# A second block's input projection in pairs of column blocks with seven products, and an SSM projection with its weights stationary

## The chip, the cores and the metric

The kernel runs on one core of a Trainium2 chip. The metric is the device time of one execution in microseconds, the median of several runs. The core has five engines with queues of their own that meet through semaphores: TensorE (PE; its weight loads are listed apart as PEld), VectorE (DVE), ScalarE (ACT), GpSimd (POOL) and SyncE (SP), which here only issues DMAs.

## The reference

Two transformer-like blocks run one after the other on 1024 tokens of width 1024, all in float32. Inputs are x, a conditioning vector and some forty weights.

The first block normalises and modulates x, projects it with `w_in`, and runs a dilated attention and a state-space branch (SSM) beside each other. The 256 SSM input columns are a slice of that projection. Both branches are gated, merged and projected, and a convolutional feed-forward layer follows.

The second block is the one that matters here:

```python
h = _rmsnorm_2(x, norm_g)
p = h @ w_in                      # 1024 x 1024 times 1024 x 7680
(u, v, z_a, x_b, b_g, c_g, z_b, x_c, z_c, g_a, g_b, g_c) = split(p)
y_a = (gmlp(u, layernorm(gelu(v))) * silu(z_a)) @ w_pa
y_b = (shortconv(x_b, b_g, c_g) * silu(z_b)) @ w_pb
y_c = (pool(x_c) * silu(z_c)) @ w_pc
merged = sigmoid(g_a) * y_a + sigmoid(g_b) * y_b + sigmoid(g_c) * y_c
out = _rmsnorm_2(x + merged @ w_o, final_g)
```

`shortconv` multiplies c_g by x_b, runs a causal convolution of width 3 over tokens and multiplies by b_g. `pool` takes causal window means of 2, 4, 8 and 16 tokens over four groups of 128 columns. `gmlp` mixes tokens in chunks of 128 with a triangular matrix per group.

## The kernel before

Precision: every float32 operand X of a large product is split into a high part (`hi`, a cast by ACT to a rounded float32 format) and a low part (`lo`, X minus hi, a subtraction on DVE or POOL). A product is three matmuls: hi·hi, hi·lo and lo·hi. `split` does this for activations and `Stream.split_to` for weights.

Layouts: `mmB` holds 128 weight columns stationary and moves 512 tokens past them, so that its result has features on partitions; a block is 8 row tiles of the contraction, 3 passes and 2 token halves, 48 matmuls. `mmA` holds 128 tokens stationary and moves 512 weight columns.

Order: the kernel is not issued as it is written. `Plan.add` (L212) records every operation, and `Plan.schedule` (L277) is a list planner: it keeps a model clock with a price for each operation (`Plan.cost`, L249), lets every engine take the first operation in the order of writing that is ready and whose buffers fit, and so fixes the order on each engine and the place of each buffer. All operations are issued at L432, so each row of the profile has that line. There are 50 SBUF tiles of 128 x 1024 ("s"), two PSUM tiles of two banks ("mm") and four of one ("tr"). Groups of buffers have caps in `nc.glim`: 5 raw weight tiles ("r") and 14 split ones ("w").

Weights: `_items` lists the weight tiles of 512 KB in the order of use. `Stream.dma_to` loads them on SP's queue, `split_to` splits them, `get` hands them out.

The stages that the change touches are these:

- "us", the SSM input projection, before the gates of the first block. For each of eight token phases it takes every eighth token as the stationary operand (a slice with a step of 8) and moves 256 weight columns: 8 x 8 x 3 matmuls. DVE copies the result to `xs`, and `ssm_gen` goes on from there, a few steps after each gate.
- "lastdown": the last feed-forward projection of the first block, its normalisation in batches of four token tiles, and `u3_tr`, the transposes to features on partitions for the second block. The first token half is transposed during the last tiles, the second during the next stage. `x2_out` sends the block's output to DRAM for the last residual.
- "A_v", "A_uz": v, u and z_a with `mmA`; gelu, layernorm and products per token tile. "spat": the token mixing and 32 transposes.
- "gateA", "B", "gateB", "C", "zc", "gc", "yc": column blocks one by one with `mmB`; each gate block is followed by its part of an output projection (`gated`), so that the gates stay in SBUF.
- "wo": the output projection, with the residual added in `proj_half`, and the last normalisation.

Of the kernel before, what the change touches and what calls it, by code (L numbers as in the profile page):

```python
# [19 lines left out]
NT = 8  # L20
# [26 lines left out]
NWARM = 14  # L47
WPOOL = set([0, 1, 2, 3])
# [20 lines left out]

def _items():  # L70
# [3 lines left out]
    for k in range(2):  # L74
        it.append(("U", "w_in", k, 1536, 256))
# [32 lines left out]
    for nm in ("v", "u", "za"):  # L108
        for k in range(4):
            it.append(("A", "w_in_2", k, o[nm], 512))  # L110
    it.append(("WS", None, 0, 0, 0))
    for n in range(0, 8, 2):
        it.append(("B", "w_in_2", n, o["ga"], 128))
        it.append(("B", "w_in_2", n + 1, o["ga"], 128))
        it.append(("P", "w_pa_2", n, 0, 0))
    for n in range(4):
        for nm in ("cg", "xb", "bg", "zb"):
            it.append(("B", "w_in_2", n, o[nm], 128))
    for n in range(0, 8, 2):
        it.append(("B", "w_in_2", n, o["gb"], 128))  # L120
        it.append(("B", "w_in_2", n + 1, o["gb"], 128))
        it.append(("P", "w_pb_2", n, 0, 0))
    for n in range(4):
        it.append(("B", "w_in_2", n, o["xc"], 128))
    it.append(("WP", None, 0, 0, 0))
    for n in range(4):
        it.append(("B", "w_in_2", n, o["zc"], 128))
    for n in range(8):
        it.append(("B", "w_in_2", n, o["gc"], 128))
    for n in range(0, 8, 2):  # L130
        it.append(("P", "w_pc_2", n, 0, 0))
# [13 lines left out]
class Plan:  # L145
# [103 lines left out]
    def cost(self, eng, method, args, kw):  # L249
# [198 lines left out]
def kernel(ctx: ExitStack, tc: tile.TileContext, x, wts, wada, vecs, rows, ssmv, wglu, ttab, iden,  # L448
# [11 lines left out]
    nc.glim = {"r": 5, "w": 14}  # L460
# [8 lines left out]
    def raw():  # L469
        return slot("r", group="r")  # L470
# [19 lines left out]
    mod = nc.own(cst.tile([128, 32], F32, name="mod"), "cst", 99)  # L490
    half = nc.own(cst.tile([128, 2], F32, name="half"), "cst", 99)
# [15 lines left out]
    x2_d = dtile("x2_d", 8)  # L507

# [57 lines left out]
    class Stream:  # L566
# [6 lines left out]
        def dma_to(self, j):  # L573
            while self.d <= min(j, len(_ITEMS) - 1):
                t = raw()
                w = _item_cols(_ITEMS[self.d])
                nc.sync.dma_start(out=t[:, :w], in_=wts[self.d][:, :w])
                self.raw[self.d] = t
                self.d += 1

        def split_to(self, j):
            while self.s <= min(j, len(_ITEMS) - 1):
                self.dma_to(self.s)
                r = self.raw.pop(self.s)
                it = _ITEMS[self.s]
# [10 lines left out]
                self.s += 1  # L596

# [60 lines left out]
    def wA(items):  # L658
        return [p for i in items for p in wA1(i)]

# [642 lines left out]
    wu = []  # L1303
    for _ in range(2):
        h, l = st.get()
        hv, lv = kview(h, 4, 256), kview(l, 4, 256)
        for k in range(4):
            wu.append((hv[:, k, :], lv[:, k, :]))
    xs = [slot("xs"), slot("xs")]
    for q in range(2):  # L1310
        ps = mm_ps()
        for j in range(4):
            s = 4 * q + j
            ws_ = []
            for k in range(8):
                h, l = u.full[k]
                ws_.append((h.rearrange("p (j s) -> p s j", s=8)[:, s, :], l.rearrange("p (j s) -> p s j", s=8)[:, s, :]))
            mmA(ps[:, 256 * j:256 * j + 256], ws_, wu)
        p3 = ps.rearrange("p (s g c) -> p s g c", s=4, g=16)
        for gh in range(2):  # L1320
            nc.vector.tensor_copy(out=xs[gh].rearrange("p (g s c) -> p s g c", g=8, s=8)[:, 4 * q:4 * q + 4],
                                  in_=p3[:, :, 8 * gh:8 * gh + 8, :])
# [276 lines left out]
    def proj_half(a, c, src, dst, row):  # L1599
# [4 lines left out]
        for t in range(NT):  # L1604
# [4 lines left out]
            if row is None and c and t == NT - 1:  # L1609
                for c_ in (slice(0, 256), slice(256, 512)):  # L1610
                    ps = tr_ps()[:, 0:256]
                    mmA(ps, xs, [(h[:, c_], l[:, c_]) for h, l in w])
                    tt(o[:, c_], ps, xr[:, c_], ALU.add)
# [4 lines left out]
            if row is None:  # L1618
                tt(o, ps, xr[:, 0:512], ALU.add)
# [166 lines left out]
    x2_of = {}  # L1786

    def x2_out(t):
        a, r = x2_of.pop(t)
        x2 = slot("x2")  # L1790
        act(x2, a, AF.Identity, scale=r)
        nc.gpsimd.dma_start(out=x2_d[t], in_=x2)

    def u3_tr(th, k):
        if (k, th) not in u.half:
            u.half[k, th] = slot("u3", F32R).rearrange("p (h n) -> p h n", h=2)
        o = u.half[k, th]
        tr_evac([xn[4 * th + j] for j in range(4)], k, o[:, 0, :], o[:, 1, :], vec("norm_g_2", k))

    for t in range(NT):  # L1800
# [13 lines left out]
        if j == 3:  # L1814
# [7 lines left out]
            ra, rb = r[:, 0:4], r[:, 4:8]  # L1822
            for jj in range(4):
                a = xn[t - 3 + jj]
                n_ = slot("xn")
                if XL[jj] == "a":
# [4 lines left out]
                x2_of[t - 3 + jj] = (a, ra[:, jj:jj + 1])  # L1831
        if t in (4, 5, 6, 7):
            u3_tr(0, 2 * (t - 4))
            u3_tr(0, 2 * (t - 4) + 1)
            x2_out(t - 4)
    del g2r, gfr, w
    fts.clear()
    nc.label = "A_v"

    lnr = slot("lnr")  # L1840
    load_in(lnr, rows[4].partition_broadcast(128))
    wv = wA([st.get() for _ in range(4)])
    vh = [slot("vh", F32R) for _ in range(4)]
    vl = [slot("vl", F32R) for _ in range(4)]
# [319 lines left out]
```

## Time and profile before

| | |
|---|---|
| median of 3 runs | 2172.23 us (2171.98 to 2172.95) |
| profiled execution | 2172.54 us |
| its span, from first to last instruction | 2170.8 us |
| instructions in the span | 24273 |
| PE busy, matmuls | 2119.2 us (98%), 9774 |
| PEld busy | 1764.2 us (81%) |
| DVE busy | 1141.4 us (53%) |
| ACT busy | 653.2 us (30%) |
| POOL busy | 267.6 us (12%) |
| mean granted clock of TensorE | 0.987 |

Busy times are of the span. A matmul's own duration in the listings covers its way through the array, and neighbours overlap; how fast they follow each other is read from a group's busy time over its count. In an operation, "s" is any SBUF tile, "mm" and "tr" are the PSUM tiles, "sm" small tiles; "out<-in" names what is written and read.

### The profile page before, as it was taken

How to read it: one execution, taken by the hardware profiler on the slowest of the kernel's cores; microseconds unless marked ns; L12 is line 12 of the kernel's file. 1: busy time of each engine (PE TensorE's matmuls, PEld its weight loads, DVE VectorE, ACT ScalarE, POOL GpSimd, SP SyncE). 2: the span in 40 equal slices, each digit the busy share in tenths (PEclk: the TensorE clock that was granted, in tenths of full speed). 3: DMA queues.
4: the chain of work that ended last, by engine and by line, in shares of the span. 5: the costliest groups of instructions: out<-in, count | busy, mean ns of one | idle time of the engine just before them, and what ended most of it. 6: DMA issues, size and time to landing. Idle time of an engine off the chain costs nothing.

```text
span 2170.8 us, 24273 instructions
## 1 busy us (share of the span) xinstructions
PE 2119.2 (98%) x9774; PEld 1764.2 (81%) x9774; DVE 1141.4 (53%) x1897; ACT 653.2 (30%) x947; POOL 267.6 (12%) x280
## 2 busy tenths in 40 slices
PE   6999989999999999999999999999999999999998
PEld 4798868888888788888887878888888888888887
DVE  8858764887673852444347587431232232540445
ACT  4402213776522433112112374221111111221312
POOL 4202421222301100000004225000000000000020
PEclk9999979999999999999999999999999999999999
DMA  8518134433652321211122221210111111111212
GB/s 322 179 67 273 68 107 107 107 85 81 251 176 83 122 88 39 78 39 59 49 88 88 68 107 49 76 60 30 59 49 39 39 58 43 51 49 39 92 54 78
DMA packets 60224, 195.15 MB, mean 90 GB/s; under 512 B 6992, under 2 KB 11440, under 8 KB 60112
## 3 DMA queue, kind: packets, MB, share of 16 engines
q1 hardware_dynamic: 40464, 136.39, 18.4%
q0 software_dynamic: 19648, 57.22, 8.2%
q8 instruction: 76, 1.25, 0.2%
q14 instruction: 36, 0.29, 0.0%
HBM read 156.29 MB, written 28.31 MB: 85 GB/s over the span
## 4 chain that ended last, share of the span: by engine, by line
PE 91%; DVE 7%; issue 1%; DMA 0%; ACT 0%; POOL 0%; SPq 0%; DVEq 0%; ACTq 0%; POOLq 0%
PE mm L432 59%; PE tr L432 32%; DVE s L432 6%; DVE sm L432 1%; ACT s L432 0%; POOL s L432 0%; DMA s<-in_wada_dram 0%; DMA gs_d<-s 0%; DVE mod L432 0%; SPq L432 0%; DVEq L432 0%; ACTq L432 0%; POOLq L432 0%
## 5 line engine op out<-in xcount | busy, mean ns | idle before, releaser
L432 PE MATMUL mm<-s,s 128*128 128x512 f32 (+1 forms) x5960 | 1381.9, 392 | 4.1 <-DVE s L432 2.0
L432 PEld LDWEIGHTS mm<-s,s 128*128 128x128 f32 x5960 | 1130.0, 194 | 230.3 <-DVE s L432 4.6
L432 PE MATMUL tr<-s,s 128*128 128x512 f32 (+4 forms) x3192 | 700.5, 377 | 12.9 <-DVE s L432 11.1
L432 PEld LDWEIGHTS tr<-s,s 128*128 128x128 f32 (+2 forms) x3192 | 561.6, 190 | 122.2 <-DVE s L432 14.0
L432 DVE TENSOR_TENSOR s<-s,s 128x1024 fp32r<-128x1024 f32 (+12 forms) x387 | 416.4, 1100 | 287.9 <-PE mm L432 223.2
L432 ACT CAST s<-s 128x1024 fp32r<-128x1024 f32 (+4 forms) x238 | 217.6, 933 | 351.7 <-DVE s L432 123.7
L432 ACT ACTIVATE s<-s 128x512 f32<-128x512 f32 (+4 forms) x139 | 120.8, 869 | 397.3 <-DVE s L432 317.7
L432 POOL TENSOR_TENSOR s<-s,s 128x512 fp32r<-128x512 f32 (+11 forms) x106 | 166.3, 1583 | 294.5 <-ACT s L432 205.8
L432 DVE SCALAR_TENSOR_TENSOR s<-s,mm 128x1024 f32<-128x1024 f32 x48 | 58.6, 1220 | 161.6 <-PE mm L432 114.7
L432 DVE SCALAR_TENSOR_TENSOR s<-s,s 128x1024 fp32r<-128x1024 f32 (+4 forms) x65 | 79.5, 1225 | 98.9 <-ACT s L432 98.5
L432 DVE TENSOR_TENSOR s<-tr,s 128x512 fp32r<-128x512 f32 (+3 forms) x114 | 72.5, 652 | 99.7 <-PE tr L432 77.2
L432 ACT ACTIVATE s<-s,sm 128x512 f32<-128x512 f32 (+7 forms) x127 | 99.4, 798 | 66.5 <-DVE sm L432 66.1
L432 ACT ACTIVATE s<-mm 128x1024 f32<-128x1024 f32 x32 | 32.9, 1028 | 259.8 <-PE mm L432 259.8
L432 PE MATMUL tr<-idn,s 128*128 128x128 f32 x560 | 83.7, 282 | 16.6 <-ACT s L432 10.4
L432 POOL DMA_DIRECT2D s<-x_d x16 | 8.8, 549 | 722.0 <-PE mm L432 721.4
L432 PEld LDWEIGHTS tr<-idn,s 128*128 128x128 f32 x560 | 68.3, 144 | 33.3 <-ACT s L432 12.9
L432 DVE TENSOR_TENSOR s<-s,tr 128x512 f32<-128x512 f32 (+1 forms) x130 | 78.8, 618 | 27.1 <-PE tr L432 19.3
L432 DVE SCALAR_TENSOR_TENSOR s<-mm,vt,s 128x1023 f32<-128x1023 f32 (+3 forms) x36 | 41.8, 1162 | 82.2 <-ACT s L432 81.7
L432 DVE TENSOR_TENSOR s<-s,mm 128x1024 f32<-128x1024 f32 (+1 forms) x26 | 29.6, 1137 | 89.0 <-PE mm L432 88.6
L432 ACT COPY s<-tr 64x256 f32<-64x256 f32 (+2 forms) x78 | 37.2, 485 | 45.4 <-PE tr L432 24.5
L432 ACT ACTIVATE s<-mm,hb 128x1024 f32<-128x1024 f32 x15 | 16.7, 1115 | 105.3 <-PE mm L432 82.0
L432 ACT ACTIVATE s<-tr 128x512 f32<-128x512 f32 (+1 forms) x44 | 25.9, 595 | 72.9 <-PE tr L432 66.9
(100 smaller groups left out, 669.8 us busy)
## 6 DMA issues: line engine op xcount, KB each, us to landing
s<-in_wts_dram SPq DMA_DIRECT2D x167, 512.0 KB, 3.7
s<-in_wada_dram SPq DMA_DIRECT2D x48, 512.0 KB, 6.1
s<-s POOLq DMA_DIRECT2D x32, 256.0 KB, 4.9
s<-in_x_dram SPq DMA_DIRECT2D x8, 512.0 KB, 9.1
v_d<-s POOLq DMA_DIRECT2D x8, 512.0 KB, 5.7
gs_d<-s POOLq DMA_DIRECT2D x8, 512.0 KB, 4.2
ga_d<-s POOLq DMA_DIRECT2D x8, 512.0 KB, 3.2
s<-in_ttab_dram SPq DMA_DIRECT2D x8, 512.0 KB, 3.9
```

Of the source, the lines that this page charges most:

```text
L432: hook(getattr(getattr(self.nc, eng), method)(*args, **kw), self.ops[i][7] + f"|{self.start[i]:.0f}|{i}")
```

## The change

Column blocks of `w_in_2` go through the second block in 30 pairs. A pair is two blocks of 128 columns, B1 and B2; the contraction of 1024 is cut into two halves and the tokens into two halves. So the product is a 2 x 2 by 2 x 2 block product, and it is done in Winograd's form of Strassen's scheme with seven products of a 512-row contraction instead of eight. The operands of activations (a11, a12, s1 to s4, a22; `Seven`) are made once. Those of weights (b11, b21, t1 to t4, b22; `Weights`) are made for each pair: POOL adds, ACT and DVE split. A product is 4 row tiles x 3 matmuls of 512 tokens. `seven` puts them together: some results are copied or added by ACT and DVE into two output tiles, and three products are accumulated onto what already stands in their PSUM bank.

The first three pairs do their two products of the first token half early (`first_halves`), before the second half is transposed. v, u and z_a now also come with features on partitions: v is transposed for its layernorm (`ln_gen`, run in steps between the pairs of "B"), and "spat" multiplies after its transposes. The gates, the branches b and c and the normalised v go to DRAM (`g2_d`, `bb_d`, `cc_d`, `vq_d`) and come back for the three output projections, which now stand at the end, one after the other. The block's output for the residual goes to DRAM unscaled, and `proj_half` scales it when it adds it.

The "us" stage uses `mmB` (two blocks of 48 matmuls with weights stationary), copies the result to SBUF and transposes it: 16 transposes that read tokens with a step of 8.

The planner's price of such a matmul goes from n/2.4 + 2.5 to (n + 32)/2.4 ns, and the caps "rr" (6 raw tiles of paired weights), "w2" (9 weight operands) and "o" (6 output tiles) are new. Raw tiles of pairs are not loaded earlier than 120 operations ahead.

```diff
@@ Plan.cost
-                return (n if n >= 256 else 4 * n) / 2.4 + 2.5
+                return ((n if n >= 256 else 4 * n) + 32) / 2.4
@@ "us"
-    for q in range(2):
-        ps = mm_ps()
-        for j in range(4):
-            s = 4 * q + j
-            ws_ = []
-            for k in range(8):
-                h, l = u.full[k]
-                ws_.append((h.rearrange("p (j s) -> p s j", s=8)[:, s, :], l.rearrange("p (j s) -> p s j", s=8)[:, s, :]))
-            mmA(ps[:, 256 * j:256 * j + 256], ws_, wu)
+    for gh in range(2):
+        ps = mm_ps()
+        mmB(ps, wB(st.get()), u, 8)
+        f = slot("us")
+        for h in range(2):
+            c = slice(512 * h, 512 * h + 512)
+            nc.scalar.copy(out=f[:, c], in_=ps[:, c])
+        ...
+                nc.tensor.transpose(out=ps[:, 128 * j:128 * j + 128],
+                                    in_=f.rearrange("p (j s) -> p s j", s=8)[:, 4 * h + j, :], identity=idn)
+            nc.vector.tensor_copy(out=x4[:, 4 * h:4 * h + 4], in_=ps.rearrange("p (s g c) -> p s g c", s=4, g=8))
@@ class Seven
+        def rest(self, ps, qs):
+            for k in ks:
+                p, q, n = ps[k], qs[k], ns[k]
+                v.tensor_tensor(out=lo(n), in0=lo(q), in1=hi(q), op=ALU.add)
+                v.tensor_tensor(out=hi(n), in0=lo(n), in1=lo(p), op=ALU.subtract)
+                put("s2", k, hi(n), v)
+                g.tensor_tensor(out=lo(q), in0=lo(p), in1=lo(q), op=ALU.subtract)
+            for k in ks:
+                put("s3", k, lo(qs[k]), g if k < 2 else v)
+            for k in ks:
+                put("s1", k, lo(ns[k]), v)
+                g.tensor_tensor(out=hi(ps[k]), in0=hi(ps[k]), in1=hi(ns[k]), op=ALU.subtract)
+            for k in ks:
+                put("a22", k, hi(qs[k]), v)
+            for k in ks:
+                put("s4", k, hi(ps[k]), g)
@@ products
+    def product(X, W, key, ps, a, b, on):
+        wh, wl = W.pop((key, b))
+        for k in range(X.nk):
+            xh, xl = X.p[a, k]
+            c = slice(128 * k, 128 * k + 128)
+            for i, (l_, r_) in enumerate(((wh, xh), (wh, xl), (wl, xh))):
+                nc.tensor.matmul(out=ps, lhsT=l_[:, c], rhs=r_, start=not on and not k and not i, ...)
+    def halves(X, W, key):
+        o1 = slot("o1", group="o")
+        pa = tr_ps()
+        product(X, W, key, pa, "a11", "b11", False)
+        nc.scalar.copy(out=o1[:, 512:1024], in_=pa)
+        yield o1
+        product(X, W, key, pa, "a12", "b21", True)
+        nc.scalar.copy(out=o1[:, 0:512], in_=pa)
+    def seven(X, W, key, o1=None):
+        ...
+        product(X, W, key, pb, "s2", "t2", False)
+        tt(c12, c21, pb, ALU.add)
+        if g:
+            next(g, None)
+        pc, pd = mm_ps()[:, 0:512], mm_ps()[:, 0:512]
+        product(X, W, key, pc, "s3", "t3", False)
+        tt(c22, c12, pc, ALU.add)
+        product(X, W, key, pd, "s1", "t1", False)
+        tt(c22, c22, pd, ALU.add)
+        product(X, W, key, pc, "a22", "t4", True)
+        tt(c21, c12, pc, ALU.add)
+        product(X, W, key, pd, "s4", "b22", True)
+        tt(c12, c12, pd, ALU.add)
+        return o1, o2
@@ start of the second block
+    pre = first_halves(X, W, range(NPRE))
+    for k in range(4):
+        u3_tr(1, k)
+    X.rest([xq[k] for k in range(4)], [xq2[k] for k in range(4)])
@@ gates
+    def gate_pairs(gd):
+        for n in range(0, 8, 2):
+            for j, g in enumerate(pair()):
+                act(g, g, AF.Tanh, scale=0.5)
+                nc.gpsimd.dma_start(out=gd[n + j], in_=g)
@@ proj_half
-                tt(o, ps, xr[:, 0:512], ALU.add)
+                stt(o, xr[:, 0:512], ra2[:, t:t + 1], ps, ALU.mult, ALU.add)
```

## Rows read from the trace of the kernel before

**Rows 1.** Page: busy us of PE, and the clock strip in 40 slices.
```profile
PE 2119.2 (98%) x9774; PEld 1764.2 (81%) x9774; DVE 1141.4 (53%) x1897; ACT 653.2 (30%) x947; POOL 267.6 (12%) x280
PEclk9999979999999999999999999999999999999999
```

**Rows 2.** Page: chain that ended last, by engine.
```profile
PE 91%; DVE 7%; issue 1%; DMA 0%; ACT 0%; POOL 0%; SPq 0%; DVEq 0%; ACTq 0%; POOLq 0%
```

**Rows 3.** Waits of PE: us in total, times, longest (first, last of eight).
```profile
PE tr L432 <- DVE s L432: 22.5, 12, 7.5
...
PE mm L432 <- DMA s<-in_wada_dram: 0.4, 1, 0.4
```

**Rows 4.** Windows: us, busy PE PEld DVE ACT POOL, PEclk, DMA share, GB/s.
```profile
96.60:142.80 46.20, 46.20 (x194) 46.20 (x194) 20.45 (x148) 3.30 (x4) 0.53 (x1) 1.00 0.39 145
...
1450.00:1700.00 250.00, 250.00 (x1104) 207.02 (x1103) 60.14 (x51) 41.91 (x41) 0.00 (x0) 1.00 0.15 47
...
285.00:335.00 50.00, 41.96 (x154) 32.53 (x152) 22.50 (x26) 9.80 (x12) 8.11 (x8) 0.69 0.34 109
1254.00:1265.00 11.00, 7.92 (x36) 6.47 (x35) 8.56 (x15) 8.70 (x13) 3.74 (x3) 0.84 0.12 48
```

**Rows 5.** Chain in order of time, a piece: start us, us, what.
```profile
848.52 43.52 PE mm L432 x192
```

**Rows 6.** Lines of PE by form, 95:165: count, busy us, mean ns.
```profile
L432 PE MATMUL mm<-s,s 128*128 128x256 f32 x192 | 46.3, 403 | 0.0
```

**Rows 7.** Timeline of PE, 1240:1330: start us, us, instruction, count, idle before.
```profile
1257.47 2.68 PE L432 MATMUL tr<-idn,s 128*128 128x128 f32 x16 [3.08 <-ACT s L432]
...
1266.21 1.03 PE L432 MATMUL tr<-idn,s 128*128 128x128 f32 x8
1267.00 5.73 PE L432 MATMUL mm<-s,s 128*128 128x512 f32 x24
```

**Rows 8.** Lines of DVE by form, whole run (first), then 1350:2150.
```profile
L432 DVE TENSOR_TENSOR s<-s,s 128x512 fp32r<-128x512 f32 x26 | 21.9, 855 | 1.6 <-ACT s L432 1.5
...
L432 DVE TENSOR_TENSOR s<-s,s 128x1024 fp32r<-128x1024 f32 x75 | 91.9, 1237 | 204.0 <-PE mm L432 199.0 <-ACT s L432 4.5
...
L432 DVE TENSOR_TENSOR s<-s,s 128x128 f32<-128x128 f32 x32 | 7.2, 286 | 0.2
...
L432 DVE TENSOR_TENSOR s<-s,tr 128x512 f32<-128x512 f32 x4 | 2.7, 684 | 0.1
```

**Rows 9.** Lines by form, whole run: DVE evacuation, ACT cast, POOL addition, issue.
```profile
L432 DVE TENSOR_SCALAR s<-tr,mod 128x512 f32<-128x512 f32 x16 | 12.5, 806 | 5.0 <-ACT s L432 4.7 <-PE tr L432 0.2
...
L432 ACT CAST s<-s 128x512 fp32r<-128x512 f32 x27 | 16.3, 618 | 8.2 <-DVE s L432 7.6
...
L432 POOL TENSOR_TENSOR s<-s,s 128x512 f32<-128x512 f32 x20 | 28.1, 1417 | 49.5 <-ACT s L432 46.0 <-DVE s L432 3.4
...
L432 POOL DMA_DIRECT2D s<-x_d x16 | 8.8, 549 | 722.0 <-PE mm L432 721.4 <-issue 0.6
```

**Rows 10.** Timeline of DVE: one 512-column low part, and the second half's scaling.
```profile
80.30 0.69 DVE L432 TENSOR_TENSOR s<-s,s 128x512 fp32r<-128x512 f32 x1 [0.71 <-ACT s L432]
...
1287.72 1.42 DVE L432 TENSOR_SCALAR s<-s,sm 128x1024 f32<-128x1024 f32 x2
```

**Rows 11.** Timeline of DVE: two idle times in "us", and the long stretch.
```profile
119.80 1.29 DVE L432 COPY s<-mm 128x512 f32<-128x512 f32 x2 [12.66 <-PE mm L432]
...
142.85 1.29 DVE L432 COPY s<-mm 128x512 f32<-128x512 f32 x2 [12.66 <-PE mm L432]
...
247.89 52.21 DVE L432 TENSOR_TENSOR s<-s,s 128x1008 f32<-128x1008 f32 x38 [1.76 <-POOL s L432]
```

**Rows 12.** Timelines of POOL and DVE about 58, and one DVE addition alone.
```profile
57.71 2.34 POOL L432 TENSOR_TENSOR s<-s,cact 128x1024 f32<-128x1024 f32 x1
...
29.79 0.41 DVE L432 TENSOR_TENSOR s<-s,s 128x256 f32<-128x256 f32 x1
...
58.21 2.11 DVE L432 TENSOR_TENSOR s<-s,s 128x256 fp32r<-128x256 f32 x1
```

More of the change, by code (lines that the diff above doesn't have):

```diff
@@ L507 @@
     x2_d = dtile("x2_d", 8)
+    bb_d = dtile("bb_d", 4)
+    cc_d = dtile("cc_d", 4)
+    vq_d = dtile("vq_d", 4)
+    g2_d = [dtile(f"g2{i}_d", 8) for i in range(3)]
     def load(o, i, eng=None):
@@ new lines, in first_halves, with early @@
+    def first_halves(X, W, keys):
+        r, last = [], None
+        for key in keys:
+            g = halves(X, W, key)
+            r.append(next(g))
+            if last:
+                next(last, None)
+            last = g
+        next(last, None)
+        return r
+    def early(n):
+        o = []
+        for i in range(n):
+            o += [("early0", i)] + [("early1", i - 1)] * (i > 0)
+        return o + [("early1", n - 1)]
+    def seven(X, W, key, o1=None):
+        g = None
+        if o1 is None:
+            g = halves(X, W, key)
+            o1 = next(g)
+        o2 = slot("o2", group="o")
+        c21, c12, c22 = o1[:, 512:1024], o2[:, 0:512], o2[:, 512:1024]
+        pb = tr_ps()
+        product(X, W, key, pb, "s2", "t2", False)
[12 more added lines that the diff above has]
+        return o1, o2
@@ L1784 @@
     xn = {}
[L1786 to L1792, printed above, removed]
-    def u3_tr(th, k):
[L1795 to L1798, printed above, removed]
+    X, xq, xq2 = Seven(4), {}, {}
+    def u3_tr(th, k):
+        s_ = slot("xq")
+        for j, kk in enumerate((k, k + 4)):
+            ps = tr_ps()
+            for i in range(4):
+                nc.tensor.transpose(out=ps[:, 128 * i:128 * i + 128], in_=xn[4 * th + i][:, 128 * kk:128 * kk + 128],
+                                    identity=idn)
+            if j:
+                ts(s_[:, 512:1024], ps, vec("norm_g_2", kk), None, ALU.mult)
+            else:
+                act(s_[:, 0:512], ps, AF.Identity, scale=vec("norm_g_2", kk))
+        if th == 0:
+            xq[k] = s_
+            X.first(k, s_)
+        else:
+            xq2[k] = s_
     for t in range(NT):
@@ L1973 @@
+    ln = ln_gen()
     nc.label = "B"
-    bb_ = Act()
     for n in range(4):
-        cg = slot("cg")
-        nc.scalar.copy(out=cg, in_=blk())
-        tt(cg, cg, blk(), ALU.mult)
+        cg, xb = pair()
+        next(ln, None)
+        next(ln, None)
+        tt(cg, cg, xb, ALU.mult)
+        next(ln, None)
         cv = slot("cv")
@@ new lines, with spilled @@
+    nc.label = "ga"
+    gate_pairs(g2_d[2])
+    nc.label = "uz"
+    ug = []
+    for n in range(4):
+        u_, z_ = pair()
+        gelu2s(u_)
+        silu2(z_)
+        tt(u_, u_, z_, ALU.mult)
+        ug.append(u_)
+    X.p.clear()
+    def spilled(src, e=None):
+        a = Act()
+        for k in range(4):
+            f = slot("sf")
+            load_in(f, src[k])
+            hi, lo = slot("bh", F32R), slot("bl", F32R)
+            split(hi, lo, f, None, e)
+            a.full[k] = (hi, lo)
+        return a
```

506 lines of the change are left out of this document (293 added, 213 removed).

## The prediction

> **What bounds the kernel now.** I read the page first. TensorE is busy 98% of the span and its clock strip is nearly all nines [rows 1], and in the chain that ended last 91% of the span is PE [rows 2]. The waits say how little else there is: the largest sum that PE waited for is 22.5 us, a third of it in one piece of 7.5 us [rows 3]. The windows then tell the stages apart. In the long second half PE is busy for the whole of 1450:1700 at full clock, while DVE is busy 60 of the 250 us and POOL none [rows 4]. So the stage that the change rewrites is bound by the number of matmuls alone, and what a matmul costs is the piece of the chain in which 192 of them take 43.52 us: 0.2267 us each [rows 5]. One stage differs: in 96.6:142.8 PEld, the weight load, is busy for all of the 46.2 us [rows 4]. The grouped lines name it: 192 matmuls of only 256 columns in 46.3 us, 0.241 us each, more than a full 512 [rows 6]. The code there loads every eighth token column as weights; what ends last is the load of a strided stationary operand, and the short moving operand cannot cover it.
>
> **The change part by part.** The sum is made against the profiled execution: 2172.54 us, a span of 2170.8 and 1.7 around it; the median of the runs is 2172.23, so nothing needs converting.
>
> *Seven products.* A pair of blocks of w_in_2 took 2 blocks x 8 row tiles x 3 passes x 2 token halves = 96 matmuls of 512 columns. It becomes 7 products x 4 x 3 = 84, of the same shape. The items "v", "u" and "za" had 3 x 8 x 24 = 576 matmuls, the 48 other blocks 48 each, 2880 in all; thirty pairs need 2520. Gone: 360 x 0.2267 = **-81.6 us**, all of it in a stretch where PE never waits [rows 4, 5].
>
> *SSM input projection.* 192 matmuls in 46.2 us become 2 blocks of 48, 96 x 0.2267 = 21.8: **-24.4 us**. The sixteen transposes that it adds are counted next.
>
> *Transposes.* 16 here, and 32 in the layernorm, which now receives v with features on partitions. (The 32 around "spat" and the 64 into the second block only change their shape or place.) 48 in all; eight cost 1.03 us, sixteen after an idle stretch 2.68 [rows 7], that is 0.13 to 0.17 each. The sixteen new ones read with a step of eight, which at worst costs what the strided load does, 0.241 [rows 6], so 6 to 10 us. I take **+7**.
>
> *The evacuations.* Per pair DVE gets 7 low parts of weight operands and 5 additions out of PSUM, ACT 7 casts and 2 copies, POOL 4 additions. Durations: a 512-column low part 0.86 us on DVE (0.69 undisturbed, below), an addition from PSUM 0.68 [rows 8]; an ACT cast 0.62 and a POOL addition 1.42 [rows 9]. DVE 7 x 0.86 + 5 x 0.68 = 9.4, ACT 7 x 0.62 + 2 x 0.62 and two tanh of 1024 columns at twice that, 8.1, POOL 5.7 and its DMA issues at 0.55 each [rows 9], beside 84 x 0.2267 = 19.04 of PE. In the gate stages (12 pairs) this is hidden. The other stages have more vector work. B adds to DVE per two pairs six operations of 1024 columns at 1.24 [rows 8], 7.4, so 3.7 a pair; its layernorm is eight statistics and eight products of 512 columns at 0.69, 32 additions of 128 at 0.29 [rows 8] and some 6 us of small operations, about 26, over its first five pairs 5 each: 18.1 beside 19.04 and 0.8 of transposes. C adds per pair on the average 2.5 window sums, a fused operation, a low part and a silu at 1.24 and two halves at 0.69, 8.2: 17.6 beside 19.04 and 6 x 0.2267. v adds two gelus, each three operations of at most 1.24, 7.4: 16.8 of 19.0. PE thus keeps its lead on the average, but in B with little to spare, and there the cap of six on output tiles bites as well: the four v tiles hold four of them until the layernorm has transposed them, so the ACT copy that opens the next pair waits for the postprocessing of this one.
>
> Three matmul groups of a pair enter a bank again (a12·b21, a22·t4, s4·b22) and wait for its reader; queued behind that wait is all of PE. Between reader and return lies one other product, 12 x 0.2267 = 2.7 us; the reader needs 0.68 and at most one 1024-column operation ahead of it, 1.24 [rows 8]: 1.9. The cover holds unless two long operations stand in front. I take **+6 us** for v, B and C together, between 0 and 26 (the rival on the port, below).
>
> *The start of the second block.* This is where a stall is new. Before, the first stage began with the first token half while the second was normalised and transposed. Now the six half products of three pairs, 72 x 0.2267 = 16.3 us, are the only work that asks nothing of the second half. In the old trace the last down-projection matmul ended at 1272.7, and the scaling of the second half's tiles until 1289.1 [rows 7, 10]: 16.4 us, which the 16.3 just cover. Then come 32 transposes (about 4.2 us), and behind them on DVE per row tile an evacuation (0.81 [rows 9]), two additions and a low part before the first new product can end: 4 x (0.81 + 3 x 0.69 [rows 10]) = 11.5 us, against 4.2 of transposes and 2.7 of the product: 4.6 us short. POOL's fourteen additions of 1.42 run meanwhile and all later operands queue behind. Cover gone altogether would be the whole 11.5 + 20 (POOL) less 10 us of PE work, some 22. I take 9, and 3 for the clock: the stretch 285:335 with its 7.5 us idle has a mean of 0.69, so much of it at 1.2 instead of 2.4 GHz, and 1254:1265 with 3.1 us idle still 0.84 [rows 3, 4, 7]. **+12 us**, between 3 and 30.
>
> *What follows the SSM projection.* PE is 24 us earlier there; is what it waits for? The 7.5 us stall near 290 stands at the end of an unbroken 52 us of DVE [rows 11]. But DVE itself sat idle 12.66 us twice, for the two halves of the projection [rows 11], and its small SSM operations are queued behind those copies. Both halves are now 10.9 us long instead of 23, so DVE's chain moves up by about as much as PE. **0**, between -8 (the stall and its slow clock shrink) and +22 (DVE does not come earlier at all).
>
> *Without a term.* 36 tiles go out to DRAM and come back (24 gates, 4 + 4 + 4): 37.7 MB over some 800 us, 47 GB/s on top of 47 at a DMA share of 0.15 [rows 4]; 36 more issues on POOL's queue at 0.55 are 20 us of its 800, on a POOL that stood idle there; the reloads go out on SP up to 300 operations ahead. The residual of the last projection is one fused DVE operation for another, and eight ACT scalings vanish from an engine with room. The planner's price of a matmul rises by 11 ns, so the order changes throughout: I take 0 and keep 5 either way, an eighth of the 43 us that PE waits in the whole run (eight rows, the first and the last are shown [rows 3]). Between the last pair and the output projections the chain of that pair (six operations on DVE, three on ACT, some 10 us) and the reloads lie beside the first of three stages of 192 matmuls, 43.5 us, whose operand is already in DRAM.
>
> Sum: 2172.5 - 81.6 - 24.4 + 7 + 6 + 12 = **2091.5 us**.
>
> **The rivals.** *A, the port.* While one POOL addition ran (57.71, 2.34 us), a 256-column DVE addition with two SBUF inputs lasted 2.11 us, where one alone takes 0.41 [rows 12]: DVE stood until POOL was through. If the two exclude each other everywhere, a pair costs 7 x 0.69 + 5 x 0.68 + 4 x 1.42 = 13.9 us of joint time [rows 8 to 10], B 13.9 + 8.7 = 22.6 against 19.8 on five pairs (+14), C 22.1 against 20.4 on four (+7), v 21.3 against 19.0 on two (+5): 26 instead of 6, and at the start 18 of DVE and 20 of POOL in series less the 13 that PE has to do, 25 instead of 12. That gives 2091.5 + 20 + 13 = 2125. Against it: most DVE operations of a pair can fall between POOL's four. The Trainium skill ("SBUF — State Buffer", "Who interferes with whom") states this as a rule: VectorE with two SBUF inputs and a GpSimd instruction that reads SBUF take one port in turn, whoever is later waiting for the whole instruction. By that rule the trace agrees where the two met; how often they will, no row of before shows.
> *B, the SSM chain keeps its time:* the DVE work between 150 and 300 is nearly unbroken at its end, and if DVE does not gain from the shorter projection, PE waits the 22 us instead: 2113. The two idle stretches of 12.66 speak against it.
> *C, the start is hidden* (PE takes products of later pairs in between) and B and C cost nothing: 2091.5 - 18 - 5 = 2068.
> *D, slower than before.* The returns into a bank come late in every pair. Thirty pairs have 90 of them; what the PE arithmetic saves net is 99 us, so 1.1 us at each return eats all of it. If every one found another 1024-column operation in front and lost 1.24, that is 112 us: 2172.5 - 99 + 112 + 12 = 2197, and the clock would fall besides. Against it: with 9 of 19 us DVE busy in the gate stages there is seldom such a queue.
>
> **How the numbers follow.** My forecast 0.57, A 0.15, B 0.10, C 0.11, D 0.07. The range 2064 to 2132 holds A, B and C at their prices, and leaves out D and mixtures of A and B. About 0.2% is what a measurement of this kernel can tell from no change: faster 0.92, the same 0.02, slower 0.06 (D, short of its mildest form).
>
> **What would show it.** Some 9,370 matmuls and loads instead of 9,774; the SSM projection about 24 us long, with PEld no longer full; the pairs 19 to 20 us apart in the gate stages. My start term is right if PE's largest new wait stands at the first product that uses both token halves, and is 5 to 12 us. If pairs in B are 22.6 us apart, it is A; if the stall near 290 has only moved to 270 and keeps its 7.5 us, B is wrong; if it grows to 20 or more, B is right. The forecast is wrong if waits of one microsecond are scattered over all pairs.

## The result and the profile after

The changed kernel takes 2123.87 us, median of four runs (2120.32 to 2126.19), beside 2172.11 for the kernel before on the same chip: a ratio of 0.978 [0.976, 0.979]. The forecast was 2091.5, so the sign and the range held and the size did not: of the 80.7 us forecast, 48.2 came. Nearly that time stood as rival A, 2125; what it had right and what not is taken up below.

The page of the profiled execution (2124.2 us) comes first: busy time of the engines, the clock strip, the shares of the chain; after it the waits of PE (us in total, times, longest).

```profile
PE 2037.1 (96%) x9366; PEld 1678.7 (79%) x9366; DVE 1365.8 (64%) x2147; ACT 746.2 (35%) x1153; POOL 499.2 (24%) x436
...
PEclk9999969999999999999999998999999999999999
...
PE 82%; DVE 13%; ACT 2%; issue 2%; DMA 1%; POOL 0%; SPq 0%; DVEq 0%; ACTq 0%; POOLq 0%
```

```profile
PE tr L442 <- DVE s L442: 39.2, 20, 7.8
PE tr L442 <- ACT s L442: 15.2, 8, 4.0
PE mm L442 <- DVE s L442: 12.1, 13, 1.9
```

There are 9,366 matmuls, as counted, against 9,774 [rows 1]. But DVE holds 13% of the chain where it held 7 [rows 2], and the largest group of PE's waits, also for DVE, is 39.2 us in 20 pieces, where it was 22.5 in 12 [rows 3]. The arithmetic went as planned; new waits took a good part of it back.

Where they are is read from windows and from PE's timeline. Windows have, as before, busy time and count of PE, PEld, DVE, ACT, POOL, then the granted clock, DMA share and GB/s.

```profile
96.80:121.90 25.10, 25.10 (x120) 21.03 (x119) 24.72 (x157) 4.74 (x7) 0.53 (x1) 1.00 0.73 267
1700.00:1880.00 180.00, 180.00 (x796) 149.14 (x795) 103.39 (x128) 73.56 (x107) 53.58 (x44) 1.00 0.29 107
...
1250.00:1300.00 50.00, 38.02 (x167) 28.32 (x165) 45.95 (x57) 29.72 (x51) 31.24 (x22) 0.90 0.21 75
1300.00:1350.00 50.00, 44.99 (x178) 36.35 (x178) 39.09 (x43) 19.32 (x30) 29.11 (x23) 0.90 0.32 115
```

The SSM projection is 25.1 us long, transposes included, with PEld at 21 of them; it was 46.2 with PEld full [rows 4], 21.1 more. In 1700:1880 PE doesn't stop at all. The stretch 1250:1350, the start of the second block, is the opposite: 345 instructions, of which 48 are transposes, would take 297 x 0.2267 + 48 x 0.13 = 73.6 us at full speed and take 100. So 26.4 us are lost there, 17.0 as idle time, the rest mostly to the clock, whose mean is 0.90 there: part of the stretch ran at 1.2 instead of 2.4 GHz. PE's timeline shows the order of events (start, us, instruction, count, idle time before):

```profile
109.34 1.04 PE L442 MATMUL tr<-idn,s 128*128 128x128 f32 x8
...
274.89 0.79 PE L442 MATMUL tr<-s,s 64*128 64x128 f32 x2 [7.85 <-DVE s L442]
...
1251.12 5.72 PE L442 MATMUL mm<-s,s 128*128 128x512 f32 x24
...
1257.46 2.30 PE L442 MATMUL tr<-s,s 128*128 128x512 f32 x9
...
1264.17 13.39 PE L442 MATMUL tr<-s,s 128*128 128x512 f32 x57 [2.00 <-DVE s L442]
1277.40 3.66 PE L442 MATMUL tr<-idn,s 128*128 128x128 f32 x32
...
1311.13 2.07 PE L442 MATMUL tr<-s,s 128*128 128x512 f32 x4 [4.98 <-DVE s L442]
```

The row at 109.34 has eight of the new strided transposes. The stall that stood near 290 is at 267 to 275 and 7.85 us long instead of 7.5: it has moved with the rest. The last down-projection ends at 1256.8, 15.9 earlier than before (1272.7, [rows 7]), though the stall's end had moved by 21.1 (296.0 to 274.9). And the 32 transposes of the second token half stand behind the 72 matmuls of the early products (from 1257.46 on, the last 57 in a row), 4.8 us after the scalings that they need were done (ACT's two ended at 1270.40 + 2.19 = 1272.6, DVE's two earlier). The rows that say so, of ACT, and what follows the transposes on DVE and POOL:

```profile
1270.40 2.19 ACT L442 ACTIVATE s<-s,sm 128x1024 f32<-128x1024 f32 x2 [1.52 <-DVE sm L442]
```

```profile
1292.84 18.24 DVE L442 TENSOR_TENSOR s<-s,s 128x512 fp32r<-128x512 f32 x14
```

```profile
1293.00 10.06 POOL L442 TENSOR_TENSOR s<-s,s 128x512 f32<-128x512 f32 x6 [0.63 <-DVE s L442]
1304.42 4.91 POOL L442 TENSOR_TENSOR s<-s,s 128x512 fp32r<-128x512 f32 x3 [1.36 <-ACT s L442]
```

DVE takes 18.24 us for 14 low parts of 512 columns, 1.30 each; one alone took 0.69 [rows 10]. POOL runs nine of its own in that stretch. PE's wait of 4.98 us at 1311.13, its largest new one, ends with DVE's last one. The prediction's sign for its start term, one wait of 5 to 12 us at the first product that uses both halves, was not met: that product starts at 1283.39 behind a wait of 2.33 us, four more of 1.3 to 2.2 follow, and the 4.98 us stand in the next pair.

### The profile page after: what moved, and what is told of

It reads as the page before. It is cut to its first block, busy times and chain, and to the rows that moved or that the text cites. A ratio compares the mean times of both kernels' runs of the same rounds, so it can differ in the third digit from the quotient of the medians.

```text
span 2122.4 us, 24495 instructions
## 1 busy us (share of the span) xinstructions
PE 2037.1 (96%) x9366; PEld 1678.7 (79%) x9366; DVE 1365.8 (64%) x2147; ACT 746.2 (35%) x1153; POOL 499.2 (24%) x436
## 3 DMA queue, kind: packets, MB, share of 16 engines
q1 hardware_dynamic: 46080, 156.83, 21.1%
## 4 chain that ended last, share of the span: by engine, by line
PE 82%; DVE 13%; ACT 2%; issue 2%; DMA 1%; POOL 0%; SPq 0%; DVEq 0%; ACTq 0%; POOLq 0%
PE mm L442 46%; PE tr L442 36%; DVE s L442 11%; ACT s L442 2%; DVE sm L442 2%; DMA gs_d<-s 0%; DMA s<-in_x_dram 0%; DMA s<-g_d 0%; POOL s L442 0%; DMA ga_d<-s 0%; SPq L442 0%; DVE mod L442 0%; DVEq L442 0%; ACTq L442 0%; POOLq L442 0%
## 5 line engine op out<-in xcount | busy, mean ns | idle before, releaser
L442 PE MATMUL mm<-s,s 128*128 128x512 f32 x5000 | 1174.4, 393 | 16.0 <-DVE s L442 12.1
L442 PEld LDWEIGHTS mm<-s,s 128*128 128x128 f32 x5000 | 940.7, 189 | 216.5 <-DVE s L442 16.9
L442 PE MATMUL tr<-s,s 128*128 128x512 f32 (+4 forms) x3696 | 832.4, 381 | 32.7 <-DVE s L442 26.4
L442 PEld LDWEIGHTS tr<-s,s 128*128 128x128 f32 (+2 forms) x3696 | 659.4, 191 | 170.9 <-DVE s L442 33.3
L442 DVE TENSOR_TENSOR s<-s,s 128x512 fp32r<-128x512 f32 (+11 forms) x569 | 579.0, 1046 | 133.8 <-ACT s L442 76.9
L442 ACT CAST s<-s 128x512 fp32r<-128x512 f32 (+4 forms) x420 | 303.6, 747 | 452.6 <-PE mm L442 171.2
L442 POOL TENSOR_TENSOR s<-s,s 128x512 f32<-128x512 f32 (+9 forms) x166 | 284.5, 1719 | 492.1 <-ACT s L442 236.4
L442 ACT ACTIVATE s<-s 128x1024 f32<-128x1024 f32 (+3 forms) x171 | 161.2, 945 | 437.7 <-DVE s L442 326.5
L442 DVE TENSOR_TENSOR s<-s,mm 128x512 f32<-128x512 f32 (+1 forms) x138 | 101.9, 738 | 124.0 <-PE mm L442 122.7
L442 DVE SCALAR_TENSOR_TENSOR s<-s,s 128x1024 fp32r<-128x1024 f32 (+2 forms) x81 | 98.7, 1224 | 97.2 <-ACT s L442 94.5
L442 PE MATMUL tr<-idn,s 128*128 128x128 f32 x608 | 89.2, 283 | 19.8 <-ACT s L442 11.0
L442 DVE TENSOR_TENSOR s<-tr,s 128x512 fp32r<-128x512 f32 (+3 forms) x97 | 61.3, 650 | 63.0 <-PE tr L442 39.2
```

What stands on the lines that cost most here:

```text
L442: hook(getattr(getattr(self.nc, eng), method)(*args, **kw), self.ops[i][7] + f"|{self.start[i]:.0f}|{i}")
```

## The experiments

All ratios are to the kernel before, timed beside each; the changed kernel itself stands at 0.978 [0.976, 0.979] on that scale.

**e1, the SSM projection alone.** The kernel before with only the new "us" stage:

```diff
-        it.append(("U", "w_in", k, 1536, 256))
+        it.append(("B", "w_in", n, 1536, 128))
...
-            mmA(ps[:, 256 * j:256 * j + 256], ws_, wu)
+        mmB(ps, wB(st.get()), u, 8)
```

> The kernel before with the SSM projection alone changed (weights stationary, 16 transposes); the planner's old price, no paired products. Theory (the two parts are independent, DVE moves up with PE): the stage takes 25 us instead of 46.4, the stall of 7.5 us stands 21 us earlier and is as long, and the time is 2172 - 21 = 2151. Rival (DVE's chain keeps its time): the stall grows by some 20 us and the time stays at 2165 to 2172.

Measured: 2150.21 us, 0.989 [0.988, 0.991], 22 us less. The half of the change that concerns the SSM holds as worked out. The rest of the change, the pairs and the planner's price, then brought 2150.2 - 2123.9 = 26.3, where the forecast has 81.6 less some 22 of costs: the miss lies there.

**e2, the combinations of the input on VectorE.** In `Seven.rest`:

```diff
-            v, g = nc.vector, nc.gpsimd
+            v, g = nc.vector, nc.vector
```

> The changed kernel with POOL's fourteen instructions in the operands of the activations (8 additions, 6 low parts) put on DVE. Theory 1 (the port: DVE's two-input operations stand while POOL adds): the 14 DVE operations that took 18.2 us fall back to about 0.6 each, DVE gains more than the 14 x 0.6 = 8.4 us that it takes over, the loss at the start falls from 27 to 18 to 22 and the time to 2115 to 2119. Theory 2 (DVE simply has too much to do): the loss rises by about 8 and the time to 2130 to 2134.

Measured: 2122.11 us, 0.976 [0.975, 0.978]: the interval overlaps that of the changed kernel, so no difference is shown, and neither number was met. The trace has the 14 low parts at their full speed:

```profile
1291.94 8.51 DVE L442 TENSOR_TENSOR s<-s,s 128x512 fp32r<-128x512 f32 x14
1300.69 8.89 DVE L442 TENSOR_TENSOR s<-s,s 128x512 fp32r<-128x512 f32 x11 [0.25 <-ACT s L442]
```

But DVE now makes 25 of them in that place where POOL had made some, and is done at 1309.6, beside 1311.1 in the change. The last down-projection ended 2.8 us later in this execution (1259.6), so counted from there DVE is 4.3 us sooner: the start gains some of what was looked for, and the stage ahead of it loses it.

**e3, the same work left out.** The additions and low parts that `Seven.rest` gives to POOL are not made:

```diff
-                g.tensor_tensor(out=lo(q), in0=lo(p), in1=lo(q), op=ALU.subtract)
...
-                put("s3", k, lo(qs[k]), g if k < 2 else v)
+                if k < 2:
+                    self.p["s3", k] = self.p["s2", k]
+                else:
+                    put("s3", k, lo(qs[k]), v)
...
-                g.tensor_tensor(out=hi(ps[k]), in0=hi(ps[k]), in1=hi(ns[k]), op=ALU.subtract)
...
-                put("s4", k, hi(ps[k]), g)
+                self.p["s4", k] = self.p["s1", k]
```

> Leaves out: the operands s3 (first two row tiles) and s4 are not made, s2 and s1 stand in for them, and the eight additions on POOL are not done; DVE does what it did before, so the output is another. Theory 1 (the port): with POOL's 14 instructions gone and DVE's count the same, the loss at the start falls from 27 to 12 to 17 us, the time to 2109 to 2114. Theory 2 (DVE's own work is the bound): the DVE operations keep their length and the time falls by no more than 3, to 2121.

Measured: 2107.71 us, 0.970 [0.968, 0.971], 1.3 below theory 1's number. VectorE's work is what it was, and it is done sooner; PE in the second window never stops:

```profile
1300.00:1350.00 50.00, 50.00 (x221) 41.09 (x221) 29.24 (x43) 17.38 (x27) 18.27 (x17) 1.00 0.44 153
```

So the fourteen instructions, with the six ACT casts that go with their low parts, cost the start and what follows up to 16 us, though PE waits for VectorE and not for POOL in the list of waits. That it is POOL's doing them is not shown by this run: in e2 VectorE did the same work, and the time stayed.

**e4, five early products instead of three.** If the start lacks cover, two more give 48 x 0.2267 = 10.9 us of it.

```diff
-NPRE = 3
+NPRE = 5
```

> The changed kernel with five pairs, not three, doing their first two products before the second token half is there: 24 x 2 x 0.2267 = 10.9 us more of cover. Theory (what is short at the start is matmuls that need nothing of the second half; the length of the chain is given): the loss falls from 27 by 8 to 11, the time to 2113 to 2116. Rival (DVE's throughput is short, and the four more weight operands, 2.4 to 3.4 us of DVE, come on top): it falls by no more than 4, to 2120 or above.

Measured: 2131.88 us, 0.981 [0.980, 0.982]: 8 us more than the change, which no theory had. PE's and DVE's timelines say why:

```profile
1291.58 3.65 PE L442 MATMUL tr<-idn,s 128*128 128x128 f32 x32
...
1325.27 4.63 PE L442 MATMUL tr<-s,s 128*128 128x512 f32 x10 [4.91 <-DVE s L442]
```

```profile
1292.65 3.37 DVE L442 TENSOR_SCALAR s<-tr,vt 128x512 f32<-128x512 f32 x4 [8.06 <-PE tr L442]
```

The transposes come at 1291.58 instead of 1277.40, behind the additional products, and DVE stands idle for 8.06 us for want of them. Behind the transposes PE's waits are nearly those of the change, the longest 4.91 us where it was 4.98. The early products do not lie beside the chain that they should cover; they are queued ahead of it.

**e5, the transposes written first.** The planner takes what is written earlier when two operations are ready:

```diff
-    pre = first_halves(X, W, range(NPRE))
     for k in range(4):
         u3_tr(1, k)
+    pre = first_halves(X, W, range(NPRE))
```

> The 32 transposes of the second half of the input are written ahead of the early products, nothing else; in the changed kernel they stand at 1277.4 us behind 72 early products on TensorE, while their inputs are there at 1272.6. Theory 1 (the early products delay the chain that they should cover): the transposes run some 5 us earlier, the additions behind them too, and the kernel takes 2118 to 2121 instead of 2123.9. Theory 2 (the start is set by VectorE and GpSimd sharing the port, however early they begin): TensorE loses at its idle before the transposes what it gains behind them; within 1.5 of 2123.9.

Measured: 2133.34 us, 0.982 [0.980, 0.983], 9.5 us more: theory 1 fell, and theory 2's number too. DVE of this kernel, DVE of the change, then POOL and PE of this kernel:

```profile
1267.09 1.21 DVE L442 TENSOR_SCALAR sm<-sm 128x4 f32<-128x4 f32 x1
...
1268.54 2.48 DVE L442 TENSOR_SCALAR sm<-sm 128x8 f32<-128x8 f32 x3
...
1272.85 0.17 DVE L442 COPY ra<-sm 128x4 f32<-128x4 f32 x1
```

```profile
1268.11 0.45 DVE L442 TENSOR_SCALAR sm<-sm 128x8 f32<-128x8 f32 x3
...
1270.40 0.17 DVE L442 COPY ra<-sm 128x4 f32<-128x4 f32 x1
```

```profile
1268.36 1.29 POOL L442 TENSOR_TENSOR s<-s,s 128x512 f32<-128x512 f32 x1
1269.73 1.26 POOL L442 TENSOR_TENSOR s<-s 128x512 f32<-128x512 f32 x1
```

```profile
1274.06 0.90 PE L442 MATMUL tr<-idn,s 128*128 128x128 f32 x3 [4.71 <-ACT s L442]
...
1315.07 5.49 PE L442 MATMUL tr<-s,s 128*128 128x512 f32 x12 [5.47 <-DVE s L442]
```

Three operations of eight columns, 0.45 us in the change, take 2.48 while POOL adds, and one of four columns takes 1.21: the normalisation's chain of tiny operations is held, from its first to the copy 7.2 us (1265.81 to 1273.02) instead of 3.1 (1267.51 to 1270.57). The scaling ends later, and PE stands 4.71 us before the first transpose. So they begin only 3.3 us sooner, and from there to the product that waited for DVE it is 41.0 us (1274.06 to 1315.07), where the change had 33.7 (1277.40 to 1311.13). Why that part became longer this trace alone doesn't settle.

**e10, both.** The transposes first and five early products:

```diff
-NPRE = 3
+NPRE = 5
...
-    pre = first_halves(X, W, range(NPRE))
     for k in range(4):
         u3_tr(1, k)
+    pre = first_halves(X, W, range(NPRE))
```

> The 32 transposes ahead of the early products as in the run that took 2133.3, with five early products instead of three. Theory 1 (early products are cover where they don't stand ahead of the transposes; 48 more matmuls are 10.9 us of it): 2121 to 2126. Theory 2 (what is late is VectorE's and GpSimd's backlog, 43 of 50 us busy, and the early products bring their own four low parts into it): 2130 to 2136.

Measured: 2119.51 us, 0.976 [0.974, 0.978], theory 1 and 1.5 below its number: 13.8 less than e5 and 12.4 less than e4. Each edit alone costs 8 to 9.5 us; the two together cost nothing, and by the medians save 4, though the interval overlaps that of the change. DVE's copy behind the normalisation, and PE:

```profile
1269.59 0.17 DVE L442 COPY ra<-sm 128x4 f32<-128x4 f32 x1
```

```profile
1270.79 0.67 PE L442 MATMUL tr<-idn,s 128*128 128x128 f32 x3 [0.77 <-ACT s L442]
...
1306.36 0.78 PE L442 MATMUL tr<-s,s 128*128 128x512 f32 x2 [4.24 <-DVE s L442]
```

The copy ends 3.3 us sooner than in e5, with no addition of POOL beside the chain, and the cover is 10.9 us larger: 14.2 in all, beside the 13.8 measured. That the two make up the gain is an argument from this sum; no run has one without the other.

**e8, the planner's old price.**

```diff
-                return ((n if n >= 256 else 4 * n) + 32) / 2.4
+                return (n if n >= 256 else 4 * n) / 2.4 + 2.5
```

> The planner's price of a matmul is again that of the kernel before, 215.8 instead of 226.7 ns for 512 columns; the change is otherwise whole. Theory 1 (the price reordered the work from 297 to 1224 us and cost the 5.2 us more of waits there): these come back to 10 us of loss and the kernel takes 2118 to 2121. Theory 2 (the order there changed because the stages before it now end 22 us sooner): the loss there stays at 14 to 16 us and the time within 1.5 of 2123.9.

Measured: 2121.27 us, 0.977 [0.975, 0.978]; the time alone shows no difference from the change. The trace does: the last down-projection ends here at 1249.4, not 1256.8.

```profile
1243.63 5.74 PE L442 MATMUL mm<-s,s 128*128 128x512 f32 x24
```

7.5 us come back ahead of the second block, more than had been lost between 275 and there. About half of it is paid again: in 1860:1930 PE waits 7.5 us for DVE instead of 4.3, and in 1880:1930 its mean granted clock is 0.90 instead of 1.00; the start loses some 2 more, and in 1350:1860 PE waits 3.3 us less.

**e6, the output's low parts on VectorE.** Four of 1024 columns, made at about 1901 to 1917:

```diff
-spilled(cc_d, nc.gpsimd)
+spilled(cc_d)
```

> The four low parts of 1024 columns that are made for the output projection at about 1901 to 1917 us are made by VectorE instead of GpSimd, nothing else. Theory 1 (the waits of TensorE at 1903 to 1930, some 5 us, are VectorE held off by these GpSimd instructions): the waits mostly go, 2119 to 2122. Theory 2 (VectorE is simply late there, whoever takes the parts): it gets four instructions of some 1.2 us more and the waits stay or grow, 2123 to 2127.

Measured: 2128.73 us, 0.980 [0.978, 0.981]. Not better, and above theory 2's number. DVE and PE of this kernel:

```profile
1913.66 1.23 DVE L442 TENSOR_TENSOR s<-s,s 128x1024 fp32r<-128x1024 f32 x1 [3.37 <-PE mm L442]
...
1915.94 5.11 DVE L442 TENSOR_TENSOR s<-s,s 128x1024 fp32r<-128x1024 f32 x4
```

```profile
1921.10 12.01 PE L442 MATMUL mm<-s,s 128*128 128x512 f32 x44 [3.77 <-DVE s L442]
```

The low parts are queued on VectorE behind an evacuation that itself waits for PE (the 3.37 us idle), and PE then waits 3.77 for the last of them. Counted by the instructions that PE has left, this kernel is level with the change with 1000 left and 3.9 us behind with 700 left: in 1860:1930 PE waits 6.1 us instead of 4.3, and its mean granted clock is 0.95 instead of 1.00. So POOL was the better place here by the trace; by the times alone the intervals still overlap.

**e7, eight output tiles.**

```diff
-NO = 6
+NO = 8
```

> Eight instead of six tiles for the outputs of the pairs, nothing else. Theory 1 (the 3.0 us wait at 1675.9 us with the half clock behind it, 5.2 us together, and smaller ones in B are pairs waiting for an output tile): these go, 2117 to 2120. Theory 2 (they are VectorE held off by GpSimd and its queue, with tiles free): the tiles change nothing, within 1.5 of 2123.9.

Measured: 2125.33 us, 0.978 [0.977, 0.980]: no difference, theory 2. The forecast's cap of six tiles does not bite. The wait before gc is of another kind, in the change:

```profile
1675.85 2.07 PE L442 MATMUL tr<-s,s 128*128 128x512 f32 x4 [3.04 <-ACT s L442]
```

```profile
1671.18 3.99 DVE L442 TENSOR_TENSOR s<-s,s 128x1024 fp32r<-128x1024 f32 x2 [0.93 <-ACT s L442]
```

```profile
1671.10 1.31 POOL L442 TENSOR_TENSOR s<-s,s 128x512 f32<-128x512 f32 x1
...
1673.00 1.63 POOL L442 TENSOR_TENSOR s<-s 128x512 f32<-128x512 f32 x1
```

Two low parts of 1024 columns, 1.24 each [rows 8], take 3.99 us beside two additions of POOL; the ACT copy that PE waits for is behind them.

**e9, the pairs without GpSimd.** The edit of e2, and the four additions for each pair's weights as well:

```diff
-            v, g = nc.vector, nc.gpsimd
+            v, g = nc.vector, nc.vector
...
-                nc.gpsimd.tensor_tensor(out=o, in0=a, in1=b, op=op)
+                nc.vector.tensor_tensor(out=o, in0=a, in1=b, op=op)
```

> All additions and low parts that the 30 pairs gave to GpSimd, those of the input's combinations and the four for each pair's weights, are made by VectorE; GpSimd keeps its DMA issues and the four low parts of the output stage. Theory 1 (the waits of the second block are VectorE held off for the length of GpSimd's instructions): VectorE takes some 120 more of about 0.6 us, but none of its own is stretched; the waits in B and before gc (some 12 us with the half clock) and part of the start's 27 us go, 2112 to 2119. Theory 2 (VectorE has too much to do in any case): it is the bound in B, the waits grow, 2126 to 2135.

Measured: 2107.99 us, 0.970 [0.969, 0.972], 15.9 us less than the change; theory 1, and 4 below its number. POOL's weight additions on the page of the change; DVE's 512-column low parts in 1320:1900, grouped (count, busy us, mean ns), of the change and of this kernel; then the start's run of them and B's window in this kernel:

```profile
L442 POOL TENSOR_TENSOR s<-s 128x512 f32<-128x512 f32 x60 | 94.4, 1576 | 120.3 <-DMA s<-in_wts_dram 77.0
```

```profile
L442 DVE TENSOR_TENSOR s<-s,s 128x512 fp32r<-128x512 f32 x193 | 162.7, 862 | 49.1 <-ACT s L442 48.2
```

```profile
L442 DVE TENSOR_TENSOR s<-s,s 128x512 fp32r<-128x512 f32 x189 | 127.8, 689 | 44.2 <-ACT s L442 44.0
```

```profile
1288.49 15.14 DVE L442 TENSOR_TENSOR s<-s,s 128x512 fp32r<-128x512 f32 x25
```

```profile
1460.00:1560.00 100.00, 100.00 (x447) 82.87 (x446) 86.29 (x146) 41.74 (x66) 4.76 (x7) 1.00 0.32 111
```

The low parts take 0.689 us where they took 0.862, and in the start 0.61 where they took 1.30. DVE has 134 instructions more in the run (2281 against 2147) and is busy only 17 us longer (1382.6 against 1365.8), since its busy time had held its waiting for POOL. In B it is now busy for 86 of 100 us, and PE for all 100; in the change PE had 96.7. What the change had lost outside the start, PE's waits of 8.0 us in 1320:1880, is 1.2 here. Counted by the instructions that PE has left, this kernel is 6.3 us ahead of the change with 3300 left, just behind the start, 11.8 with 2000 left and 16.0 with 1000: more than half of the gain lies behind the start. One thing these runs do not separate: POOL's additions took 1.58 us and VectorE's take 0.69 here, so the operands are also ready sooner, whether or not VectorE was held.

**e11, three edits.** The edit of e2, that of e8, and the scaling out of PSUM on ScalarE:

```diff
-            if j:
-                ts(s_[:, 512:1024], ps, vec("norm_g_2", kk), None, ALU.mult)
-            else:
-                act(s_[:, 0:512], ps, AF.Identity, scale=vec("norm_g_2", kk))
+            act(s_[:, 512 * j:512 * j + 512], ps, AF.Identity, scale=vec("norm_g_2", kk))
```

> Three edits together: the input's combinations wholly on VectorE (2122.1 alone), the planner's old price (2121.3 alone) and the scaling of the input's upper half out of PSUM on ScalarE instead of VectorE (eight of 0.75 us, four of them in the start). If they add up: 2115 to 2119. If the planner's order decides and each shift is paid back elsewhere: 2120 to 2126.

Measured: 2109.43 us, 0.971 [0.970, 0.973], 14.4 less than the change. The first two alone had shown nothing, 1.8 and 2.6 by their medians. They do not add up to it. Either each edit is worth more where the others have relieved another late engine, or the scaling is worth most of the 10 us that are left; it was not measured alone.

**e12, all that helped.** The edits of e9, e8 and e10 and the scaling of e11:

> The pairs wholly without GpSimd (2108.0 alone), the planner's old price and the scaling on ScalarE (together with part of the first edit 2109.4), and the transposes ahead of five early products instead of behind three. By the losses of the single runs: 63 us before 1180 as with the old price, some 18 in the start and 8 behind it: 2094 to 2101. If the early products' own parts only lengthen VectorE's backlog at the start: 2102 to 2108.

Measured: 2087.75 us (2086.03 to 2088.66), 0.961 [0.959, 0.962]: 36 us less than the change, better than either number expected, and the fastest of all kernels here. Windows, and PE's timeline:

```profile
1250.00:1300.00 50.00, 43.73 (x203) 34.74 (x202) 47.41 (x86) 37.76 (x67) 2.35 (x3) 0.97 0.32 106
1300.00:1350.00 50.00, 50.00 (x214) 41.11 (x213) 36.80 (x60) 20.16 (x30) 4.26 (x8) 0.96 0.49 162
```

```profile
1270.42 17.73 PE L442 MATMUL tr<-s,s 128*128 128x512 f32 x77
1287.99 5.60 PE L442 MATMUL mm<-s,s 128*128 128x512 f32 x24
1297.80 1.22 PE L442 MATMUL tr<-s,s 128*128 128x512 f32 x2 [4.21 <-ACT s L442]
```

The transposes are done by 1270.7, 101 matmuls follow without a gap, and one wait of 4.21 us is left. It is not at the first product of both halves: into "tr" banks 132 matmuls have gone before it, 120 of them early, so the first pair's first such product has run, and the 24 into "mm" are its next two. By this count the wait is the second pair's. In the two windows PE is busy 93.7 of 100 us instead of 83.0.

## Why the prediction was right in sign and 32 us short in size

*Seven products, -81.6: right.* 9,366 matmuls against some 9,370, and in 1700:1880 796 instructions take 180.0 us, 0.226 each.

*SSM projection, -24.4, transposes +7, what follows 0: right.* 21.1 us shorter with its 16 transposes (eight in 1.04 us, so the strided reading cost nothing: the lower end of 0.13 was true), the stall near 290 moved and kept its length, and e1 gave -22. Rival B is wrong: DVE's two idle times are gone with the long projection (24.72 of 25.10 us busy).

*The start, +12: the step that failed.* It lost 26.4 in 1250:1350: 17.0 of idle time where the working has 9, and 9.4, mostly clock, where it has 3. Two parts of the working were wrong. The early products, "the 16.3 just cover", took 19.9 us (1257.46 to 1277.40), with waits of 0.75 and 2.00 us for DVE among them, and the chain's own transposes stand behind them on the same engine: these came 4.8 us after their inputs. With two more early products (e4) they came another 14 later, and the waits behind them were hardly shorter; with the transposes first (e10) the same five products gave 12.4 us. And DVE's 0.69 for a low part, with POOL's additions "meanwhile", was priced as if the two ran side by side: it was 1.30, and 0.61 with POOL's additions elsewhere (e2, e9). Neither correction alone brought the time back: the transposes first cost 9.5 us (e5), the low parts at full speed gave nothing clear of noise in the kernel's time (e2). How the 14.4 us over the 12 divide between the two is open. The upper bound of 30 did hold it.

*Evacuations in v, B and C, +6: too small, for the reason of rival A.* PE waited 8.0 us in 1320:1880, and had some half clock behind the longest wait. e9 took this to 1.2 and left DVE busier, so the amount of VectorE's work was not the reason; that it was held, or that POOL's slower additions came late, both end with e9. The two other reasons given decided nothing: eight output tiles change no time (e7), and of rival D's ninety late returns there are at most eight, which is how many waits PE has in 1320:1880.

*The planner's price, 0 ± 5: inside its bounds in the time, at their edge in its stage.* 5.2 us were lost between 275 and 1257, and e8 gets back 7.5 by there; of these its time shows 2.6, which is within the noise. *The output projections, no term:* 4.3 us of waits in 1860:1930; the low parts come late in VectorE's or POOL's queue (e6).

Adding up: 14.4 in the start, 6.2 ahead of it (the last down-projection ended at 1256.8, where the forecast's terms make 1272.7 - 24.4 + 2.3 = 1250.6), 4.3 in the output, and 2 in v, B and C over the 6: 27 of the 32 us. The last 5 are not assigned. Half clock is little of it: behind the longest wait the change has

```profile
1650.00:1700.00 50.00, 46.77 (x199) 37.98 (x198) 33.79 (x39) 21.32 (x33) 18.76 (x16) 0.97 0.32 116
```

and a mean of 0.97 over 50 us is 1.5 us.

*Rival A, the port,* gave 2125, and the number was partly luck. Its start, 25 us, is near the 26.4 measured, though e9 gives back only 6 there. Its pairs are not near: 26 us in v, B and C, where PE waited 8.0, and pairs in B were not 22.6 us apart: 425 instructions in 1460:1560, where 447 fit without waits (e9), stretch 19.8 to about 20.8. The rest of its 33 us over the forecast was made up by what it does not name: the stretch ahead of the start, the output and what is not assigned. All that POOL's share costs over VectorE's doing it is 15.9 (e9). So the prediction's argument against it ("most DVE operations of a pair can fall between POOL's four") held for most pairs, and failed at the start, where DVE worked for 18.2 us and POOL for 15 at the same time. The Trainium skill ("SBUF — State Buffer", "Who interferes with whom") says that the two take the port in turn, for whole instructions. By that rule the trace nearly agrees as far as additions and low parts go: 14 x 0.61 and nine of POOL at about 1.28 make 20 us in series, and it took 18.2.

## What to carry to other kernels

Work that is to cover a wait must not stand ahead of the waiting chain's own instructions in its engine's queue: with five early products the order was worth 12.4 us (e4, e10). But read the trace again after such an edit. With three early products the same order cost 9.5 (e5), where POOL's additions then fell on the normalisation. Before work is given to a second engine, ask for each stage whether the two work at the same time there: PE never stopped in 1700:1880, where VectorE was busy for 103 of 180 us, and POOL's share cost some 16 us elsewhere. And edits on one late chain need not add up: e4 and e5 alone cost 8.0 and 9.5 us, and together they cost nothing.

## What was not expected of the hardware

VectorE's operations of four or eight columns can be held for over a microsecond when POOL adds: three of 128x8 took 2.48 us instead of 0.45 (e5). One such chain of tiny operations, the normalisation, decided there when TensorE could go on. A busy share does not show this: the stretched instruction counts as busy, so VectorE took over 134 instructions, over 90 us at 0.69, for 17 us of busy time. And transposes that read every eighth column ran at 0.13 us each, though a stationary load of the same stride had set 0.241 in [rows 6].
